# Moving a fifth of a shifted copy through SBUF, interleaved with direct HBM copies in one DMA ring

## The chip, the cores and the metric

The kernel runs on one core of a Trainium2 chip. The metric is device time in microseconds (us), the median of several executions; the "span" of a profile is one execution seen by the hardware profiler and is 1.6 to 1.8 us shorter. Stretches, packets and idle times are those of the one execution that was traced, ratios those of all executions. The result and the experiments ran on three chips on which the kernel before takes 810.9, 819 and 822 to 823 us. Such differences are as large as some effects here, so kernels are compared by ratio to the kernel before on the same chip, or by traces of the same chip. I call them the first, second and third chip.

## The reference

```python
x = np.random.randn(8192, 8192).astype(np.float32)   # 268.4 MB
out = np.fft.ifftshift(x)                            # both axes rolled by half
```

Output row `r` is input row `(r + 4096) % 8192` with its two 16 KB halves exchanged. Nothing is computed: 16,384 half rows of 16 KB change their places.

## The kernel before

Everything is copied from HBM to HBM directly, without touching SBUF. The DMAs go out from two engines, SyncE and ScalarE, each with a queue of its own (q10 and q1 of the page); the text calls what one DMA engine has waiting in such a queue its ring. A DMA is carried out as packets, here of 4 to 16 KB, by the 16 DMA engines.

```python
ENGINES = 16
STEP = 4
...
blocks = [(1024, 16)] * 8
base = 0
for rows, per in blocks:
    dims = [[STEP * C, ENGINES], [STEP * ENGINES * C, per], [1, hc]]
    for row in range(base, base + STEP):
        src_row = (row + hr) % R
        for eng, h in ((nc.sync, 0), (nc.scalar, hc)):
            eng.dma_start(out=..., in_=...)      # 4 MB: 16 packets of 16 KB per DMA engine
    base += rows
```

## Time and profile before

| | before |
|---|---|
| median, first chip | 810.88 us |
| span of the profile | 809.3 us |
| through the DMA engines | 268.4 MB, 332 GB/s |
| HBM traffic (read and written) | 536.9 MB, 663 GB/s |
| 16 KB packets: shortest / mean | 608 / 785 ns |

There are no compute instructions to speak of, so only the DMA parts of the page matter; the prediction below shows and reads them. The rate through the engines counts a byte once per pass through a DMA engine. The rate of the HBM counts a direct byte twice, since it is read there and written there, but a byte of a load or a store once. The difference between these two rates is what the change turns on.

### The profile page before, as it was taken

The page shows a single profiled execution, that of the slowest core. Times are in us where ns is not written, and L with a number is a line of the kernel's source. Part 1 is how long each engine was busy: PE and PEld are TensorE (multiplying, and loading weights), DVE is VectorE, ACT ScalarE, POOL GpSimd, SP SyncE. Part 2 cuts the span into 40 slices and gives each one's busy share as a digit, 9 for nine tenths or more (in the row PEclk, how much of TensorE's full clock was granted, in tenths as well). Part 3 has the DMA queues.
Part 4 walks back from the last instruction along what each step waited for, and adds up shares of the span by engine and source line. Part 5 has one row for each costly group of instructions (what it writes and reads, how often), then busy time and mean ns, then how long its engine had stood idle before and what let it go on. Part 6 is the DMA issues. An engine that isn't in the chain of part 4 may idle for free. (4 is left out here: it accounts for less than half of the span.)

```text
span 809.3 us, 109 instructions
## 1 busy us (share of the span) xinstructions
POOL 0.2 (0%) x4
## 2 busy tenths in 40 slices
POOL 0000000000000000000000000000000000000000
DMA  9999999999999999999999999999999999999998
GB/s 309 327 333 332 331 337 336 325 337 336 334 331 329 332 333 337 331 337 331 334 331 332 334 330 336 334 335 330 334 332 331 337 332 337 333 339 329 334 336 300
DMA packets 17408, 268.44 MB, mean 332 GB/s; under 512 B 1024, under 2 KB 1024, under 8 KB 1024
## 3 DMA queue, kind: packets, MB, share of 16 engines
q10 hardware_dynamic: 8704, 134.22, 49.9%
q1 hardware_dynamic: 8704, 134.22, 49.5%
HBM read 268.44 MB, written 268.44 MB: 663 GB/s over the span
## 5 line engine op out<-in xcount | busy, mean ns | idle before, releaser
L54 POOL MEMSET const-bfloat16-1.0<- 128x1 bf16 x1 | 0.1, 101 | 0.0
L54 POOL MEMSET const-uint8-127<- 128x1 uint8 x1 | 0.1, 101 | 0.0
L54 POOL MEMSET const-float32-0.0<- 128x1 f32 x1 | 0.1, 98 | 0.2 <-issue 0.2
L54 POOL MEMSET const-float32-1.0<- 128x1 f32 x1 | 0.1, 98 | 0.0
## 6 DMA issues: line engine op xcount, KB each, us to landing
out_dram<-in_x_dram ACTq DMA_DIRECT2D x32, 4096.0 KB, 100.7
out_dram<-in_x_dram SPq DMA_DIRECT2D x32, 4096.0 KB, 100.6
```

The lines of the kernel that those rows point to most:

```text
L54: nc = _bacc.Bacc("TRN2", target_bir_lowering=False, num_devices=1)
```

## The change

The intent: if the HBM is over-asked, some of the rows may go through SBUF, and these staged packets will keep the DMA engines busy while asking less of the HBM at a time. Three rounds of 512 rows (18.75% of the bytes) are loaded in 0.5 MB pieces with 4 KB per partition and later stored; each such DMA is followed in the same ring by one direct DMA of 1 MB. The last 512 rows are direct copies alone.

```diff
-    for row in range(base, base + STEP):
-        src_row = (row + hr) % R
-        for eng, h in ((nc.sync, 0), (nc.scalar, hc)):
-            eng.dma_start(...)
+SLOTS = 8
+PIECES = 4
+ROUNDS = 3
...
+    for turn in range(ROUNDS):
+        loads, stores = staged(blocks.pop(0))
+        for store in (False, True):
+            copies = direct(blocks.pop(0), 512) + direct(blocks.pop(0), 512)
+            for i, (o, s) in enumerate(stores if store else loads):
+                slot = i // PIECES
+                if i % PIECES == 0:
+                    if store:
+                        q.wait_ge(loaded[slot], 16 * PIECES * (turn + 1))
+                    elif turn:
+                        q.wait_ge(stored[slot], 16 * PIECES * turn)
+                q.dma_start(out=o, in_=s).then_inc(
+                    stored[slot] if store else loaded[slot], 16)
+                q.dma_start(out=copies[i][0], in_=copies[i][1]).then_inc(copied, 16)
+                n += 1
+    while blocks:
+        for o, s in direct(blocks.pop(0), 512):
+            q.dma_start(out=o, in_=s).then_inc(copied, 16)
...
```

## The prediction

> **What bounds the kernel now.** I read the page first, because a kernel that only moves data has almost nothing on its compute engines. The second part of the page gives the DMA engines' busy share and rate in 40 slices; the third gives the queues and the HBM traffic.
>
> ```profile
> span 809.3 us, 109 instructions
> DMA  9999999999999999999999999999999999999998
> GB/s 309 327 333 332 331 337 336 325 337 336 334 331 329 332 333 337 331 337 331 334 331 332 334 330 336 334 335 330 334 332 331 337 332 337 333 339 329 334 336 300
> DMA packets 17408, 268.44 MB, mean 332 GB/s; under 512 B 1024, under 2 KB 1024, under 8 KB 1024
> q10 hardware_dynamic: 8704, 134.22, 49.9%
> q1 hardware_dynamic: 8704, 134.22, 49.5%
> HBM read 268.44 MB, written 268.44 MB: 663 GB/s over the span
> ```
>
> The reader is to see three things. The 16 DMA engines are never idle: 49.9% + 49.5% = 99.4% of their time is inside packets. The rate is flat at 325 to 339 GB/s from the second slice to the last but one, so there is no bad stage to mend. And each byte counts twice in HBM, read once and written once, so 332 GB/s of copying is 663 GB/s of HBM traffic.
>
> Then the issuing side, to exclude it: the sync queue's own waits, and the issues with their time to landing.
>
> ```profile
> SPq L34 <- DMA out_dram<-in_x_dram: 686.6, 28, 25.0
> ...
> out_dram<-in_x_dram ACTq DMA_DIRECT2D x32, 4096.0 KB, 100.7
> out_dram<-in_x_dram SPq DMA_DIRECT2D x32, 4096.0 KB, 100.6
> ```
>
> SyncE sleeps 686.6 us of 809 because four of its 4 MB copies are always in flight: queued work is never short. A copy lands 100 us after its issue because eight of them (32 MB) share 332 GB/s.
>
> Last, the packets themselves, from the trace's packet records. There are 16,384 data packets of 16 KB, 1,024 for each DMA engine. The shortest took 608 ns; 28% of them took 608 to 612 ns, the median was about 755, the mean 785 and the 95th percentile about 1,100. 16,384 B in 608 ns is 26.9 GB/s, in 785 ns 20.9 GB/s. So an engine has a floor of about 610 ns a packet, and on average 785 − 610 = 175 ns are lost to something that it shares with the others. Over 1,024 packets the floor is 625 us and the loss 179 us; with about 5 us at the ends this is the span of 809. The floor isn't what the change can lower; the loss is.
>
> **What the Trainium skill says.** "DMA: Bandwidth & Descriptors", section "Where 436 GB/s comes from", gives 435.2 GB/s for 16 ports, 27.2 GB/s each: the 26.9 GB/s of the shortest packets agrees, the mean of 20.9 is below it. "HBM Reference", section "Specifications (TRN2)", gives about 716 GB/s for the HBM of a core pair: the 663 GB/s here are 93% of it, so the HBM is the natural suspect for the 175 ns. "DMA: Bandwidth & Descriptors", section "iDMA fabric — 4 AXI ports for 8 engines, asymmetric across TPBs", has two cores' load streams together at about 702 GB/s, pure reading; no run here shows that yet. The same page, section "Issuing engines are not separate DMA queues", says that issuing from several engines concurrently only saves issue time; the two queues' shares, which sum to one engine's time, agree.
>
> **The change part by part.** *What moves.* Three rounds of 512 rows of 32 KB, 50.3 MB of 268.4 (18.75%), go HBM to SBUF and SBUF to HBM. They pass the DMA engines twice: 268.4 + 50.3 = 318.8 MB, 19% more engine work. The HBM's own traffic stays 536.9 MB, since each byte is still read once and written once. What changes is how much an engine asks of the HBM at a time: a direct packet asks for two bytes per byte moved, a load or a store for one.
>
> *Engine floor.* Per engine 218.1 MB / 16 / 16 KB = 832 direct packets at 610 ns = 507 us, and 2 × 50.3 MB / 16 / 4 KB = 1,536 staged packets. An estimate for 4 KB from the 608 ns is 152 ns, with a few ns of packet cost 155: 238 us. Floor 745 us, where it was 625.
>
> *HBM.* 536.9 MB at the 663 GB/s of now is 810 us, at the skill's 702 is 765 us, at its 716 is 750 us. One pair (8 staged and 4 direct packets on each engine) takes 8 × 155 + 4 × 610 = 3.68 us at the floor and asks the HBM for 16 × (32.8 + 131.1) KB = 2.62 MB, thus 713 GB/s; direct copies alone ask for 16 × 32.8 KB / 610 ns = 860 GB/s. So the mix brings the demand down to just what the memory can give at best: floor 745 and HBM 750 us balance. That is clearly the intent.
>
> *Issue.* The first eight issues in the trace take 0.6 to 0.9 us each. The new kernel has 96 loads, 96 stores and 208 direct copies of 1 MB, all on SyncE: 400 × 0.6 = 240 us of issue time (400 × 0.9 = 360), spread over some 800. It lies beside the transfers.
>
> *Waits.* A store of a slot waits for four loads that are a whole phase earlier in the same ring: between them lie 32 pairs of 1.5 MB, 50 MB, over 110 us at any rate above. A load of the next round waits for stores equally far back. I expect no bubble, only SyncE sleeping. At the end one block of 16 direct copies is left, so both ends cost what they cost now, some 5 us.
>
> *Sum.* 745 floor + 5 ends + what stays of the loss. The direct packets have 832 × 175 = 146 us of loss if each is slowed as before: 896 us. If the lower demand took all loss away: 750 us. To break even at 809, 59 us may stay, 71 ns a direct packet; to be 2% faster, 45 us, 54 ns. So the loss per direct packet has to fall to a third while the HBM moves slightly more than 663 GB/s.
>
> **The rivals.** (1) *The loss comes from over-asking*: too many requests at once make HBM accesses collide (read and write in turn), and at a demand of 713 instead of 860 it works better. For: 28% of the packets run at the floor even now, so the memory isn't evenly full, and collisions are what varies. The traffic is also less evenly mixed, 60% reads in load phases and 60% writes in store phases. Then 680 to 700 GB/s, 770 to 790 us. (2) *The HBM is simply full at 663 with reads and writes mixed*: then total bytes decide, 810 us at the least. For: 93% of the stated peak, and a rate flat within 2%. (3) *A soft limit*: with less asked, less is delivered, about 630 to 645 GB/s, since no engine can now make up for the wait of another: 832 to 852 us. For: the floor of 745 leaves only 8% of slack. (4) *The loss belongs to a direct packet*, whose read and write hinder each other, whatever the rest does: 896 us. Against: 28% of them show none. (5) A bound by SyncE's issue or by the slot waits: 240 to 360 us of issue and 110 us of distance speak against it; it would add tens of us.
>
> **Range and chances.** From the numbers alone 2 and 3 are the plainer readings. What draws me to 1 is the exact balance of 745 and 750 us: one staged piece of 0.5 MB for one direct of 1 MB is the ratio that a useful relief of the HBM would call for, and fine interleaving in one ring is what would hold the demand even in time. That is a judgement about the design, not a measurement. I put 0.44 on faster, 0.22 on within 2%, 0.34 on slower. The time that I name is 793 us: 745 + 5 + 43 of loss, 52 ns per direct packet, HBM at 677 GB/s. The range is 762 (nearly no loss) to 850 (the soft limit).
>
> **What would show it.** Right: direct packets with a mean near 660 ns instead of 785, staged packets at 150 to 160 ns, busy shares still at 9 in every slice, an HBM line of 670 or more, and the mixed stretches moving near 318.8 MB / 790 us = 400 GB/s through the engines, against the 332 of the last block. Wrong: staged packets well above 160 ns or direct ones above 700 (rival 3 or 4), an HBM line of 663 again (2), slices under 9 or a load or store issue ending a wait of the engines (5). The last block of direct copies alone is a control within the trace: if it moves at another rate than 332, the single ring itself matters.

## The result, and the profile after

The changed kernel takes 823.13 us (821.19 to 824.81), the kernel before 810.88 us (810.21 to 811.08). The ratio is 1.0154, with a 95% interval of 1.0134 to 1.0174: 1.5% slower, inside the 2% band. Ratios here are the mean time of one kernel's fast runs over that of the other's of the same rounds, so not quite the quotient of the medians.

The page of the changed kernel: its span, the busy tenths and the rate of the DMA engines in 40 slices, the one ring, the HBM traffic, and the issues with their median time to landing.

```profile
span 822.4 us, 451 instructions
DMA  9999999999999999999999999999999999999996
GB/s 360 396 397 400 399 403 406 395 396 389 396 391 386 402 397 401 393 393 406 392 394 393 395 392 391 391 396 399 399 398 400 395 393 390 392 391 391 347 322 237
DMA packets 44291, 318.82 MB, mean 388 GB/s; under 512 B 6400, under 2 KB 6400, under 8 KB 30976
q1 hardware_dynamic: 44288, 318.79, 100.0%
HBM read 268.44 MB, written 268.44 MB: 653 GB/s over the span
out_dram<-in_x_dram SPq DMA_DIRECT2D x208, 1024.0 KB, 23.1
stage<-in_x_dram SPq DMA_DIRECT2D x96, 512.0 KB, 23.7
out_dram<-stage SPq DMA_DIRECT2D x96, 512.0 KB, 23.8
```

The engines do move more, as intended: about 396 GB/s instead of 333. But they have 318.8 MB to move instead of 268.4, and the HBM line fell from 663 to 653. The last slice is new: its busy digit is 6 where it was 8, its rate 237 where it was 300.

The slot waits are out of it. SyncE's own waits have one line for DMAs, the final one; no slot wait appears:

```profile
SPq L56 <- DMA out_dram<-in_x_dram: 45.6, 1, 45.6
```

SyncE wasn't asleep, as the prediction had it, but held in its issues: by the trace the 400 of them took 756 us, 1.9 us each on the mean, where the first eight took 0.4 to 1.0. They still ran ahead of the engines, whose share is 1.01 in the mixed stretch (below), so the issue isn't the bound either.

Stretches near the end, first of the changed kernel, then of the kernel before; the last two columns are the busy share of the DMA engines and their GB/s.

```profile
100.00:700.00 600.00, 0.00 (x0) 1.00 1.01 396
780.00:800.00 20.00, 0.00 (x0) 1.00 1.01 324
800.00:810.00 10.00, 0.00 (x0) 1.00 0.93 318
810.00:820.00 10.00, 0.00 (x0) 1.00 0.56 226
```

```profile
400.00:600.00 200.00, 0.00 (x0) 1.00 1.00 333
790.00:800.00 10.00, 0.00 (x0) 1.00 1.00 338
800.00:810.00 10.00, 0.00 (x0) 1.00 0.72 241
```

The kernel before works at full share until its last packet ends at 808. In the changed kernel the share sinks from 800 us on: some engines have finished, others still have work. From the packet records I add up each engine's idle time in the last 40 us before the last packet's end and take the mean of the 16; I call this the idle end. It is 0.5 us before and 5.4 us after.

The rest of the difference is in the mixed stretch. By the packet records between 20 and 740 us the HBM moved 659.3 GB/s there (staged bytes once, direct bytes twice); the kernel before moved 666.2. Of the 536.9 MB of HBM traffic, 503.3 MB are in the mixed stretch: 503.3/659.3 − 503.3/666.2 ms = 7.9 us. With 4.9 us of idle end this makes 12.8 of the 13.1 us between the spans.

A third view is packet durations, for the whole kernel:

| packets | before | after |
|---|---|---|
| direct, 16 KB | 16,384, mean 785 ns | 13,312, mean 663 ns |
| staged, 4 KB | none | 24,576, mean 174 ns (shortest 156, median 159) |

The direct packets did get much faster, nearly to their floor of 610. The kernel still didn't, as the additional packets took up what was won.

### The profile page after: what moved, and what is told of

It reads as the page before. It is cut to its first block, busy times and chain, and to the rows that moved or that the text cites.

```text
span 822.4 us, 451 instructions
## 1 busy us (share of the span) xinstructions
POOL 0.2 (0%) x4
```

## The experiments

The first theory after the result: the HBM gives some 660 GB/s whatever the mix, and on top of that the mixed stretch drives the DMA engines apart, so that they finish unevenly. The second half comes from the semaphore records; a semaphore is a counter that here each DMA engine raises by one when its part of a DMA has landed. A slot is filled or emptied by four DMAs that together make 64 increments. The time from the first to the last of them was 14.4 us for the first slot; at the end of the three load phases it was 19.3, 25.3 and 28.4 us. The ring order is the same each time, so about 14 us of that is engines getting out of step. Before, the 16 increments of one DMA lay within 1.8 us of each other from beginning to end (median 1.1).

### Is it the single ring? Direct copies alone in it

Edit:

```diff
-ROUNDS = 3
+ROUNDS = 0
```

(and the final wait for stores dropped, since there are none).

> All rows direct, in 1 MB copies on the one ring; nothing is staged. Theory (the HBM gives about 660 to 668 GB/s whatever the mix, and the 13 us come from the mixing: slightly less HBM traffic in the mixed stretch, 658 instead of 667 GB/s, and DMA engines that drift 14 us apart in the load phases and so end unevenly): 806 to 813 us, engines within 2 us of each other at the end, direct packets at 785 ns mean. Rival (the single ring with its small copies costs the time): 820 us or more and a long tail here too.

Measured: 820.54 us against 818.89 on this second chip, ratio 1.0022 (1.0005 to 1.0038). Its page:

```profile
span 818.0 us, 303 instructions
q1 hardware_dynamic: 20480, 268.45, 99.3%
HBM read 268.44 MB, written 268.44 MB: 656 GB/s over the span
```

The idle end is 0.7 us. One ring and 1 MB copies cost 0.2% (by the interval at most 0.4); the rest comes from mixing. (The absolute range in the expectation was for the first chip.) In the middle of the run it moves 330 GB/s, thus 660 GB/s of HBM traffic, the measure for the runs of this chip.

### Is it the phases? Loads and stores interleaved

Edit: half of the slots are loaded while the other half is stored; copies and ratio stay. In outline:

```diff
-for turn in range(ROUNDS):
-    ... all 32 loads with 32 direct, then all 32 stores with 32 direct
+for k in range(len(units) + 1):          # a unit is half a round
+    for i in range(HALF * PIECES):
+        load piece i of unit k,      one direct copy
+        store piece i of unit k - 1, one direct copy
```

> The same pieces and the same ratio, but loads of one half of the slots alternate with stores of the other half, so that there are no phases of loads or stores alone. Theory (the drift arises in the load phases, where reads are 60% of the traffic): the last 13 us of the queue keep a DMA share over 0.7 instead of 0.44, the engines end within 3 us, 811 to 817 us. Rival (the drift belongs to staging as such, or isn't what costs the time): 820 to 825 us with the same tail.

Measured: ratio 1.0156 (1.0139 to 1.0172), just the changed kernel's. The end is even worse:

```profile
810.00:820.00 10.00, 0.00 (x0) 1.00 0.74 274
820.00:828.00 8.00, 0.00 (x0) 1.00 0.23 98
```

The idle end is 8.4 us. My idea that the load phases drive the engines apart has fallen; it is the mixture as such.

### Packet size or order: 16 KB pieces, and groups of four

Edit of the first: `PIECES = 1`, so one 2 MB load or store (16 KB packets) is followed by four direct copies. The second keeps the 4 KB pieces and only takes this order:

```diff
-    q.dma_start(out=copies[i][0], in_=copies[i][1]).then_inc(copied, 16)
-    n += 1
+    if i % 4 == 3:
+        for c in copies[i - 3 : i + 1]:
+            q.dma_start(out=c[0], in_=c[1]).then_inc(copied, 16)
+            n += 1
```

> Pieces of 16 KB: one 2 MB load or store followed by four direct copies; same bytes and ratio. Theory (the HBM decides the mixed stretch): 817 to 824 us; the floor of the staged packets falls by about 25 ns per 16 KB (4 x 159 to 611), but their loss grows, the mixed stretch stays at 390 to 398 GB/s. Rival (the engines' packet costs decide): 384 x 25 ns = 10 us less, 811 to 814 us, mixed stretch over 400 GB/s.

> The same copies as in the changed kernel, but four 0.5 MB pieces and then four direct copies in the ring instead of one and one. The packet sizes stay 4 KB and 16 KB. Theory (the engines run through their rings nearly in step, so coarse alternation makes the demand on the HBM swing between some 430 and 860 GB/s, and time with too little demand isn't made good): as the run with 16 KB pieces, 1.024 to 1.034, mixed stretch 375 to 390 GB/s. Rival (the 16 KB size of the staged packets was what cost): 1.013 to 1.018 as with one and one.

Measured: 1.0294 (1.0262 to 1.0326) and 1.0365 (1.0344 to 1.0387). For the first both theories were wrong, since neither had thought of the order. The second shows that the order is enough; it lies even above the 1.034 that its theory allowed. Its stretch from 50 to 150 us, and below it the same stretch of the kernel with one round (told below), which is on the same chip and has there still the order of the changed kernel:

```profile
50.00:150.00 100.00, 0.00 (x0) 1.00 1.01 370
```

```profile
50.00:150.00 100.00, 0.00 (x0) 1.00 1.01 396
```

The busy share is the same in both lines, yet one moves 6.6% less. At the floor (159 and 611 ns), all engines in staged packets of 4 KB can ask some 410 GB/s of the HBM, all in direct ones 860. The packet records show that the demand swings: cut into 2 us, the share of the engines' packet time that is in staged packets goes from 0 to 1 and back in this stretch, and the HBM traffic between 238 and 854 GB/s, with a mean of 613; in the kernel with one round the share stays between 0.26 and 0.42, and the mean is 660. So the engines are in the same part of their rings at the same time, and the HBM doesn't make good later what it was not asked for.

It is the worst stretch of the run. From 400 to 700 us the share stays between 0.07 and 0.69, and the grouped order nearly draws level with the run with interleaved phases, which is shown second:

```profile
400.00:700.00 300.00, 0.00 (x0) 1.00 1.01 390
```

```profile
400.00:700.00 300.00, 0.00 (x0) 1.00 1.01 394
```

A coarse order thus costs most while the engines are in step.

### What the HBM gives for what is asked: other ratios

Edit of the first: each piece of 0.5 MB is followed by 0.5 MB direct (`[64 * C, 2]` in the dims); of the second: by 0.75 MB (`[64 * C, 3]`). The direct copies left over come at the end.

> Each staged piece of 0.5 MB is followed by only 0.5 MB direct, the rest of the direct copies come at the end; same bytes. At the floor (8 x 159 + 2 x 611 ns) the mixed stretch asks the HBM for only 631 GB/s, under its limit. Theory: the loss per packet nearly goes (direct mean under 640 ns, staged under 168), the stretch is bound by the engines at 600 to 630 GB/s of HBM traffic, and the rest runs at 332 GB/s of direct copying: 830 to 850 us. Rival (the HBM loses by the staging itself, whatever is asked): the staged packets stay at 174 ns or more and the stretch stays under 600 GB/s, over 855 us.

> Each piece of 0.5 MB is followed by 0.75 MB direct, so at the floor (8 x 159 + 3 x 611 ns) the mixed stretch asks the HBM for 675 GB/s, just above what it gives. Theory (delivered is the smaller of asked and about 660, a few per cent less at the knee): 640 to 656 GB/s of HBM traffic in the mixed stretch, between the 637 and 656 of the other two ratios, ratio 1.012 to 1.022. Rival (a mix that asks just enough lets the HBM work better): over 662 GB/s in the stretch, ratio 1.010 or less.

Measured: 1.0299 (1.0283 to 1.0314) and 1.0174 (1.0137 to 1.0211). The rate of the first in 40 slices:

```profile
GB/s 356 429 419 428 422 429 420 425 421 428 421 427 422 428 421 422 423 427 422 428 421 428 400 333 329 327 324 328 326 332 327 328 331 332 329 329 333 328 329 237
```

The first half is what the DMA engines can do: 424 GB/s, direct packets at 612 ns and staged at 159 ns on the mean, which is the floor. The loss is gone there and the engines are the bound. Then come the direct copies left over, bound by the HBM. The second chip's traces give this table (asked: bytes of one pair over its floor time; delivered: from the packet records):

| direct per 0.5 MB piece | asked of the HBM | delivered | ratio |
|---|---|---|---|
| direct copies alone | 860 GB/s | 660 | 1.0022 |
| 1 MB (interleaved phases) | 705 | 656 | 1.0156 |
| 0.75 MB | 675 | 652 | 1.0174 |
| 0.5 MB | 631 | 636 | 1.0299 |

(For 1 MB and a floor of 159 and 611 ns: 2.62 MB / 3.72 us = 705. The last row delivers slightly more than asked, since packets overlap by a per cent or two: the busy share reads 1.02.) On the mean of a stretch the HBM gives what is asked up to about 640 GB/s and never more than some 660; only for some 10 us at a time, in the direct parts of the grouped order, do the records show more (about 700, for 2 us up to 854). Asking less than 860 didn't make it better at any of these ratios. (The ratio of the 0.75 MB run contains an uneven end: its traced execution, the slowest of four, has an idle end of 11.6 us.) Hence the staged share can't win: the HBM bytes are unchanged, and it is full already.

### Finer alternation: two rings

Edit: the staged DMAs in 8 KB pieces go out from ScalarE, the direct ones from SyncE, so that each DMA engine serves two rings. In outline:

```diff
-PIECES = 4
+PIECES = 2
...
-q.wait_ge(...)   q.dma_start(out=o, in_=s)            # pieces, then one direct copy
+nc.scalar.wait_ge(...)   nc.scalar.dma_start(out=o, in_=s)
...              # all direct copies in q's own loop
```

> The staged copies in 8 KB pieces on the other ring (issued from ScalarE), the direct ones on SyncE's: if an engine takes packets from the two rings in turn, 8 KB and 16 KB packets alternate one by one, with the same ratio of bytes as in the changed kernel and no coarse alternation. Theory (uneven demand costs the 1.2% in the mixed stretch): HBM traffic of the mixed stretch up from 656 to 660 to 668 GB/s, ratio 1.002 to 1.012 depending on the tail. Rival (the granularity of one and one is already fine enough): 652 to 658 GB/s, 1.013 to 1.020. In no case clearly faster than before, since the bytes of the HBM stay the same.

Measured: 1.0126 (1.0109 to 1.0144), mixed stretch 655 GB/s of HBM traffic, idle end 4.4 us. The two rings do alternate one by one: when the last staged packet starts, each engine has had 768 staged packets and on the mean 764 direct ones. The ratio lies below that of the changed kernel, but the intervals overlap, and the rate isn't what the theory wanted, 660 or more; on this point the rival holds. Uneven demand explains the coarse orders, not what is left at one and one.

### Dose: one round

Edit: `ROUNDS = 1`; twelve blocks of direct copies follow instead of one.

> One staged round instead of three, then direct copies for the rest: a dose test. Theory (the HBM gives about 660 GB/s at any mix that asks for more; the mixed stretch is some 1.2% below the rate of direct copying, and engines that drifted apart in it end unevenly): about a third of the steady cost, 3 us, and the long direct stretch lets the engines draw level again as they stay level in direct copying, so idle time at the end under 2 us: ratio 1.003 to 1.007. Rival (the drift is kept to the end whatever follows): 1.009 to 1.012 with a tail of 4 us or more. Rival (a fixed cost of the staging construct, such as the start): 1.013 or more.

Measured: 1.0122 (1.0105 to 1.0139), so a third of the dose has four fifths of the effect. The direct stretch after the mixed one, and the same stretch of the kernel without staging on this chip:

```profile
350.00:600.00 250.00, 0.00 (x0) 1.00 1.00 327
```

```profile
350.00:600.00 250.00, 0.00 (x0) 1.00 1.00 331
```

Long after the last staged packet, the same direct copies are about 1% slower, and the idle end is 4.3 us. Something that the mixed stretch caused outlives it by 550 us; the theory's recovery in the long direct stretch is refuted, and the rival that the drift is kept to the end fits. Nothing staged is left by then, but the engines may still be out of step. That is the second theory: **engines out of step move less and end unevenly, and direct copies alone don't bring them back.**

### Undoing it: a wait after the mixed stretch

Edit to the kernel with one round:

```diff
+q.wait_ge(copied, 16 * n)
+for sem in stored:
+    q.wait_ge(sem, 16 * PIECES * ROUNDS)
 while blocks:
```

> The kernel with one staged round (ratio 1.0122), but after the mixed stretch SyncE waits until every copy has landed before it issues the remaining direct copies, so that all engines start them together. Theory (engines that are out of step move less through the HBM and end unevenly): the direct stretch goes back from 326 to 329 to 331 GB/s and the idle time at the end from 4.3 to about 1 us; the wait costs some 6 to 8 us once, so the ratio is 1.004 to 1.012. Rival (the slower direct stretch has another cause, such as the rows or the buffer in SBUF): 326 GB/s as before, and the wait comes on top: 1.018 to 1.022.

Measured on the third chip, where the kernel before takes 823.39 us: 1.0105 (1.0088 to 1.0122), idle end 0.4 us instead of 4.3, direct stretch 328 GB/s. Ratio and end are as the theory expected, the rate just short of its 329 to 331, which were meant for the second chip. The end is mended beyond doubt. Whether the rate is, this comparison can't say, since the run without the wait was on another chip.

### Making it without staging: skewed direct copies

Edit to the direct kernel: the first 128 half rows go out in DMAs of 15, 14, 13 ... rows, which use only so many of the DMA engines (save the last, of one row, which the records show as 16 packets of 1 KB).

```diff
+for k in ks:                       # 15, 14, 13, 12, 10, then 11, 9, 8, 8, 7 ... 1
+    dims = [[C, k], [1, hc]]
+    stairs.append((ap(out, r, h, dims), ap(x, (r + hr) % R, hc - h, dims)))
...
+for o, s in stairs + rest:
```

> Direct copies alone, nothing staged, but the first 128 half rows go out in copies that use 15, 14, 13 ... engines, so that each engine starts the regular copies about one packet later than its neighbour, some 10 us between first and last. Theory (being out of step is what costs, not the staging): 324 to 328 GB/s in the middle where the same copies in step move 330, and 4 to 7 us idle at the end, ratio 1.012 to 1.024 where in step it was 1.0022. Rival (out of step is harmless in direct copies): 329 to 331 GB/s, ratio 1.006 to 1.011 by the tail alone. Rival (direct copies bring engines back into step): 329 to 331 and idle under 1.5 us at the end, 1.002 to 1.006.

Measured: 1.0096 (1.0081 to 1.0111), 328 GB/s in the middle, idle end 0.8 us. By their letter the rate fits the theory, the ratio the rival "harmless" and the idle end the rival "back into step"; in truth the run tests nothing. The trace shows 8.5 us of idle time in the first 20 us, 6 us more than in the plain direct kernel: the small copies went into empty rings, the engines waited for each issue, and all began the regular copies together. It is a control for a better run: the same copies without skew.

### The changed kernel again, and other rows for the engines

Edit of the first: none. Of the second: direct copies alone, but the 16 engines take 16 neighbouring rows (`[[C, 16], ...]`) instead of every fourth row.

> The changed kernel itself, on the chip of the experiments, so that its stretches can be set beside theirs. Both theories: ratio 1.013 to 1.018, mixed stretch 391 to 396 GB/s, 4 to 7 us idle at the end.

> Direct copies alone in one ring, but the 16 engines work on 16 neighbouring rows (32 KB apart) instead of every fourth row (128 KB apart). Theory (what the HBM gives depends somewhat on how the addresses of the engines stand to each other, which is also why being in step matters): a rate that differs from 330 GB/s by 1% or more either way, ratio outside 0.995 to 1.009. Rival (only the bytes count): 329 to 331 GB/s, 1.000 to 1.005.

Measured: 1.0172 (1.0144 to 1.0200) with 390 GB/s in the mixed stretch and an idle end of 5.1 us, and 1.0112 (1.0076 to 1.0148) with 323.5 GB/s in the middle (its traced execution is the slowest of four). The neighbouring rows carry the same bytes in packets of the same size, and move 1.8% less than the 329.3 that the plain direct kernel moves on this chip (below). The first is as expected, its rate at the lower edge. The second is outside the rival's range and as the theory had it, but it doesn't show the theory's cause, which was that the HBM's rate depends on how the addresses in flight lie to each other. By the measure of step at the end of the next part, the engines of this run fall partly out of step on their own (1.4 us from 20 to 100 us, 2.1 us from 300 to 790 us; 1.1 to 1.2 us in the plain direct kernel). The lines of those two stretches, first of this run, then of the plain direct kernel:

```profile
20.00:100.00 80.00, 0.00 (x0) 1.00 1.00 325
300.00:790.00 490.00, 0.00 (x0) 1.00 1.00 323
```

```profile
20.00:100.00 80.00, 0.00 (x0) 1.00 1.00 327
300.00:790.00 490.00, 0.00 (x0) 1.00 1.00 329
```

So at most the early gap, under 1%, can be put down to the rows alone; whether addresses are the reason why step matters isn't shown.

### The skew put right, and all on one chip

The last four run on the third chip. The first is the skewed kernel with its uneven copies behind 16 regular ones, so that the rings hold a backlog:

```diff
-for o, s in stairs + rest:
+for o, s in rest[:16] + stairs + rest[16:]:
```

The other three are the direct kernel, the one-round kernel and the one with the wait, unchanged.

> Nothing staged; the uneven copies stand behind 16 regular ones in the rings, so that the engines really get out of step by up to some 10 us. Theory (out of step alone lowers the rate): 0.6% or more below the direct kernel of this call in the middle, and 3 to 6 us idle at the end; ratio 1.009 to 1.018. Rival (harmless): the rate of the direct kernel within 0.3%, only the idle end: 1.004 to 1.008. Rival (direct copies restore step): idle under 1.5 us at the end, 1.001 to 1.004.

> Direct copies alone in one ring, nothing skewed, as the measure for the other three on this chip. All theories: 1.000 to 1.005, under 1 us idle at the end.

> One staged round, then direct copies. Theory (out of step costs): direct stretch 0.8% or more below that of the direct kernel of this call, 4 us idle at the end, ratio 1.010 to 1.014. Rival (the difference was chance): direct stretch within 0.4%, ratio under 1.009.

> The same with the wait for all copies after the mixed stretch. Theory: direct stretch within 0.3% of the direct kernel of this call, under 1 us idle at the end; what is won there (0.8 to 1.2% of some 550 us, and 3.5 us at the end: 8 to 10 us) about pays for the wait of 6 to 8 us: ratio 1.007 to 1.012, at most that of the run without the wait. Rival (the direct stretch is slow for another cause): 0.8% or more below, ratio 1.016 to 1.022.

| | ratio (95%) | direct stretch, 300 to 790 us | 16 landings within | idle end |
|---|---|---|---|---|
| direct | 1.0012 (1.0005 to 1.0019) | 329 GB/s | 1.2 us | 0.6 us |
| direct, skewed in the queue | 1.0269 (1.0249 to 1.0288) | 321 GB/s | 2.9 us | 4.7 us |
| one round | 1.0142 (1.0092 to 1.0192) | 326 GB/s | 2.8 us | 3.9 us |
| one round, then the wait | 1.0096 (1.0081 to 1.0111) | 328 GB/s | 1.1 us | 0.4 us |

"16 landings within" measures the step. All direct copies raise one semaphore, 16 times for each full DMA, and in a direct stretch 16 increments land in every 3.2 us. In step, those of one DMA come close together; out of step, they are spread over the whole 3.2 us. The increments from 300 to 790 us are cut into runs of 16, starting where the runs are shortest, and the table has their median length.

The lines for the stretch from 300 to 790 us, one fence for each kernel in the order of the table:

```profile
300.00:790.00 490.00, 0.00 (x0) 1.00 1.00 329
```

```profile
300.00:790.00 490.00, 0.00 (x0) 1.00 1.00 321
```

```profile
300.00:790.00 490.00, 0.00 (x0) 1.00 1.00 326
```

```profile
300.00:790.00 490.00, 0.00 (x0) 1.00 1.00 328
```

The skewed kernel settles that step matters. It stages nothing and makes the very copies of the earlier skewed run, in another order; that one moved 328 GB/s with its engines together (16 landings within 1.4 us), this one 321 with its engines apart, for 700 us without recovering. Within the run, too, it moves 326 GB/s from 20 to 60 us, while 16 landings still lie within 1.0 us, and 319 to 322 after that. The effect is larger than the theory expected (1.018 at most). Its idle end is no evidence, since it is by construction: the skewed copies leave the first engine fifteen 16 KB packets more than the last and seven more than the mean, by estimate 4.3 us at 611 ns each.

The two runs with one round say the same on a smaller scale. The wait takes the idle end from 3.9 to 0.4 us, the landings from 2.8 to 1.1 us, and the rate about half of the way from 326.4 to 329.3 GB/s, to 327.9. The end is as the theory expected; the rate is 0.4% below the direct kernel's, where the theory allowed 0.3, and far from the rival's 0.8. The wait itself costs 4.0 us of idle engines. Whether it wins on the whole isn't shown: its ratio, 1.0096, is below 1.0142, but the intervals overlap.

## Why the prediction was wrong

**What held.** The bound was read rightly: no view shows a limit at the issue or at the slot waits, though SyncE spent its time held in issues (756 us, where 240 to 360 were estimated) and not asleep. The direct packets were foretold at a mean near 660 ns in the changed kernel and took 663. There is luck in this, since the figure was what 793 us left for them, and it was no sign of being right: the run with interleaved phases has 660 ns and is 1.6% slower. Still, "the loss comes from over-asking" is true of the direct packets: where less is asked, they run near their floor, and where 631 GB/s are asked they run at it.

**The term that was mis-sized.** The sum was "745 floor + 5 ends + what stays of the loss", where the loss was charged to the direct packets alone and the staged ones were set at their estimated 155 ns. They took 174 ns. That is 1,536 × 19 ns = 29 us per engine, practically the whole distance between 793 and 823. (The longer end, below, comes on top; packets that overlap by a per cent, the share of 1.01, make up for it.) About 4 ns of the 19 are the floor, which is 159 and not 155 (6 us), since the "few ns of packet cost" were no measurement; 15 ns are loss (23 us). A staged packet also waits: its median is the 159 of the floor, but one in twenty took over 245 ns.

**The step that failed.** It is the choice among the rivals: rival 1, that the HBM works better "at a demand of 713 instead of 860", with 677 GB/s for the predicted time. Rival 2, "the HBM is simply full at 663 with reads and writes mixed", was right. The mixed stretch moved 659 GB/s where the kernel before moved 666, and at four ratios on one chip the HBM never gave more than some 660 on the mean of a stretch, however little over that was asked. The 28% of packets at the floor had been my evidence for slack; the traces show that such packets occur in a full HBM. What argued for rival 1 was, as the text said, a judgement about the design: the balance of 745 and 750 us. It set the engines against the 716 GB/s that the prediction takes from "HBM Reference", while the kernels before and after reached 672 at most over any 50 us.

**Rival 3**, less delivered when less is asked, was also partly right, but its size was off: 652 to 659 GB/s near the knee, not 630 to 645.

**What no part of it had.** Engines get out of step in the mixed stretch. Being out of step alone lowers the rate of direct copies (329 to 321 GB/s in the skewed run), and in the runs with one round it lasts to the end and leaves it uneven (3.9 us, 0.4 with the wait). "Both ends cost what they cost now, some 5 us" failed by 4.9 us. The prediction's control, "if it moves at another rate than 332, the single ring itself matters", would have misled: the last block did move at 324, but the single ring by itself costs 0.1 to 0.2%. How much of the 1.0% deficit of the mixed stretch is due to being out of step and how much to the lower demand isn't separated. Why the mixture drives the engines apart, while direct copies of every fourth row keep them within 1.8 us although they lose more time per packet, and those of neighbouring rows do so less well, is open too: the order of loads and stores isn't the cause, and the traces don't name the engines.

**No version beat the kernel before.** It is bound by 536.9 MB of HBM traffic at 666 GB/s with its engines in step and ending together. Every mixture keeps the bytes and gives up one of the other two.

## What to carry to other kernels

First find out what a wait is for: if the memory is full by bytes, easing the DMA engines or moving bytes along another path that crosses the same memory as often can't gain. When a loss per packet is taken off one kind of packet, ask whether the kinds that are added will bear it instead. And with large streams over all DMA engines, look at how evenly they end; a few microseconds of skew cost 0.9% (one round) to 2.6% (skewed copies) of the rate for the rest of these kernels, and where a natural pause exists, one wait for all copies puts the engines together again.

## What the Trainium skill lacked or had wrong

- "HBM Reference" gives the stack's rate and what a core alone can stream, but not what reads and writes mixed reach. The nearest is a row of "DMA: Bandwidth & Descriptors", section "Latency and other measured facts", where copies between HBM tensors in another layout have 214 GB/s per direction as their full rate. Copies from HBM to HBM by one core here reached 329 to 333 GB/s on the three chips, thus 659 to 666 GB/s of traffic, and no mix with staged copies exceeded that of its chip.
- "DMA: Bandwidth & Descriptors" has a cost of about 3 cycles per packet inside an engine for small descriptors, and some 10.5 ns per packet in its smallest measured transfer. It says neither of larger packets. Here the usual shortest packets of 4, 8 and 16 KB took 159, 309 and 611 ns by their records, which fits 8 ns for each packet and 27.2 GB/s for its bytes.
- No page says that DMA engines out of step move less: 321 instead of 328 GB/s for the same copies, for 700 us, or how to see it (16 landings within 2.9 instead of 1.4 us).
- No page says that the order of one-sided and two-sided copies in a ring matters: the same copies in groups of four instead of one and one ran at a ratio of 1.037 instead of 1.015 to 1.017, and lost most while the engines were in step (370 instead of 396 GB/s from 50 to 150 us).
